# Three norm stages of a one-core transformer block: the norm's products leave GpSimd, and its gain or shift is applied by rows while the transposed tile is split

## The chip, the cores and the metric

The kernel runs on one core of a Trainium2 chip. The metric is the device time of one execution in microseconds (us). Before the change it is 1857.02 us, the median of three runs (1854.01 to 1859.16).

## The reference, cut to what matters

The program computes a two-layer attention block and, on its output, a second block: an even mixer (attention over tokens and a context, and a pooling branch), a mixture of experts (moe 0), an odd mixer (gate and convolution) and a second mixture of experts. x has 512 tokens of 1024 values. The change touches three norms, each of which feeds a matrix product:

```python
def rms_norm(x, g):                      # before layer 2 of the first block
    y = x * lax.rsqrt(jnp.mean(x * x, axis=-1, keepdims=True) + EPS)
    return y * g

def first_block(x, norm_g, w_in, ..., final_g):
    for layer in range(DEPTH):
        h = rms_norm(x, norm_g[layer])
        p = h @ w_in[layer]
        ...
    return rms_norm(x, final_g)          # its output is the x of the second block

def modulate(x, gain, shift, scale):     # before the even and before the odd mixer
    return rms_norm_2(x, gain) * (1 + scale) + shift
```

At the layer boundary the norm has a gain vector and no shift. At the two mixers it has a product vector A = gain * (1 + scale) and a shift vector. The even mixer's norm stands behind the first block's last norm, so there the square sums of x and of x * final_g are both taken.

## The kernel before, in words

The 512 tokens lie in four tiles of 128 tokens by 1024 features, tokens on the partitions. A norm of a tile takes these steps: ScalarE (ACT) squares it and sums the squares; VectorE (DVE) makes the inverse root from the sum by a chain of tiny dependent instructions (`rsqrt_steps`, L376 to L398; DVE executes everything in program order); a product with the vectors follows. The normed tile is then turned: `norm_steps` (L407 to L419) transposes it with TensorE (PE), four 128x128 blocks into one PSUM bank of 128x512, two banks a tile (L414), and `split_to` (L400 to L402) splits each bank in two halves of lower precision: ACT copies the bank into `hT[0]` (hi, L401), and DVE subtracts hi from the bank and writes `hT[1]` (lo, L402). Both are one 128x512 instruction a bank. A product of such operands is three matmuls: hi by hi, hi by lo, lo by hi (L350 to L352).

The three places:

- **Place 1, layer boundary** (`block1_layer`, from L505, 495 to 545 us of the span). `square` (L509) squares on ACT (L512) and has GpSimd (POOL) multiply x with a gain gB that is broadcast to 128 partitions (L513); `turned` (L518) scales that product by the inverse root on ACT (L519). Between them PE finishes layer 1's output product (`w3_`, with DVE's additions at L668), and PE's first products of layer 2 (`latents`, 24 matmuls of 336 columns a tile) follow each tile.
- **Place 2, even mixer** (L1130 to L1245, 985 to 1032 us). `squares(i, engine)` squares x (L1144), multiplies x with final_g in place (L1146; tiles 0 and 1 on DVE, 2 and 3 on POOL), squares again (L1148) and has POOL multiply with A (L1150). `rms` ends with one DVE instruction, product times inverse root plus shift (L1161), where shift is broadcast to 128 partitions. The stage loads ax, gB, pw, ic and psc on SyncE's queue (SP) and scales psc by constants on DVE (L1179, four instructions of 128x1). PE has the last quarter of layer 2's output product (`k.w3`), the context's keys (`project`) and the keys of each tile (`normal`) between the transposes.
- **Place 3, odd mixer** (end of moe 0, L1955 to L2001, 1449 to 1494 us). `added` adds the experts' result (L1968), squares, and multiplies with A1 (tile 0 on DVE, 1 to 3 on POOL); `normed` does product times inverse root plus shift on DVE (L1977).

The order of instructions on all five engines is written by hand in these stages: inside `tc.manual_schedule` the program order is the order of issue, and generators are interleaved by `both` (one step of each in turn), `slow` (one step, then n-1 pauses) and `islice` (the next n steps). Loads go through eight DMA lanes in rotation; an issue on a lane waits for the lane's load before it. `brow` loads a vector of the modulation from DRAM to all 128 partitions.

Of the kernel before, what the change touches and what calls it, by code (L numbers as in the profile page):

```python
# [9 lines left out]
F32 = mybir.dt.float32  # L10
# [222 lines left out]
EARLY = ("e4", "ss2", "rs_y2", "rs_h2", "rs_u2", "T", "V", "ax", "gB", "psc", "pw", "ic", "ss40")  # L233
# [37 lines left out]
class K:  # L271
# [135 lines left out]
    def norm_steps(self, xn, hT, i):  # L407

        nc = self.nc
        for q in range(2):  # L410
# [7 lines left out]
            self.split_to(hT[0][:, ks, c0 : c0 + P], hT[1][:, ks, c0 : c0 + P], src)  # L418
# [32 lines left out]
def block1_layer(k, L, x, hT):  # L451
# [677 lines left out]
def even_mixer(k, x, rows):  # L1129
# [7 lines left out]
    A, sh = brow(k, rows[0], 1), brow(k, rows[0], 0)  # L1137
    us, sss, rss = {}, {}, {}

    def squares(i, engine):  # L1140
# [5 lines left out]
        engine.tensor_tensor(xi, xi, fgB, ALU.mult)  # L1146
        yield
        nc.scalar.activation(u, xi, AF.Square, scale=float(D ** -0.5), accum_out=ss[:, 1:2])  # L1148
        yield
        nc.gpsimd.tensor_tensor(u, xi, A, ALU.mult)  # L1150

    def rms(i):
# [8 lines left out]
        v.scalar_tensor_tensor(us[i], us[i], rss[i][:, 1:2], sh, op0=ALU.mult, op1=ALU.add)  # L1161
# [16 lines left out]
    for b in range(4):  # L1178
        v.tensor_scalar(psc[:, b : b + 1], psc[:, b : b + 1], 0.5 ** (b + 1), None, op0=ALU.mult)  # L1179
# [40 lines left out]
    turned = lambda i: k.norm_steps(us[i], hT, i)  # L1220
    with k.tc.manual_schedule(engines={ENG.PE, ENG.SP, ENG.Pool, ENG.Activation, ENG.DVE}):
        run(project(0))
        k.w3[0]()
        run(squares(0, v))
        k.w3[1]()
        s1, s2, s3 = squares(1, v), squares(2, nc.gpsimd), squares(3, nc.gpsimd)
        both(rms(0), chain(slow(k.w3[2](lambda g: g), 4), islice(s1, 2)))
        run(islice(s2, 2))
        run(s1)
        run(s2)  # L1230
        p1 = project(1)
        both(rms(1), rms(2), chain(slow(k.w3[3](lambda g: g), 2), slow(islice(p1, 1), 2), turned(0)))
        run(islice(s3, 2))
        n0, n1, n2, n3 = (normal(i) for i in range(4))
# [253 lines left out]
def router(k, L):  # L1488
# [7 lines left out]
    for c in range(8):  # L1496
# [6 lines left out]
         "Ab", "pos", "pos16", "most", "over", "oh", "row", "spread", "lgT", "ix", "ws", "vinf", "vpos", "ivx", "ivw",  # L1503
# [13 lines left out]
def moe(k, L, x, tables, out):  # L1517
# [265 lines left out]
    with tc.manual_schedule(engines={ENG.PE, ENG.Pool, ENG.Activation, ENG.DVE}):  # L1783
# [36 lines left out]
        if out is None:  # L1820
            k.next = brow(k, k.rows[1], 1, ("mv", 3)), brow(k, k.rows[1], 0, ("mv", 3))
# [136 lines left out]
    A1, sh1 = k.next  # L1958
# [14 lines left out]
    def normed(i):  # L1973
        v.scalar_tensor_tensor(us[i], us[i], rss[i], sh1, op0=ALU.mult, op1=ALU.add)
# [120 lines left out]
```

## Time and profile before

| | |
|---|---|
| median of three runs | 1857.02 us |
| profiled execution, its own time | 1858.75 us |
| its span | 1857.0 us |
| mean granted TensorE clock | 0.956 |
| busy PE / weight loads / DVE / ACT / POOL | 92 / 72 / 73 / 42 / 15 % |

The profile shows one execution: busy time is the time in which an engine executes, the span is the time from the first instruction to the last. PE can queue matmuls, so two rows of PE that stand one behind the other overlap a little; the distance of their starts is what one costs. A wait on a semaphore is shown as idle time, with the instruction that ended it.

### The profile page before, as it was taken

The numbers are of one execution on the slowest core, as the hardware profiler recorded it, in microseconds if no ns is written. First come the engines' busy times: TensorE is split into PE (matmuls) and PEld (weight loads), VectorE is DVE, ScalarE is ACT, GpSimd is POOL, SyncE is SP. The second block draws the span as 40 slices with busy tenths as digits, with TensorE's granted clock in tenths as the row PEclk, the third lists the DMA queues.
The fourth block names the chain that finished last, engine by engine and source line by source line (L and its number), as shares of the span: only waits on it lengthen the run. The fifth ranks groups of instructions, "written<-read, shape, count | busy, mean of one in ns | idle before, by whom it ended". The sixth has DMA issues, their size and how long they took to land. (4 is left out here: it accounts for less than half of the span.)

```text
span 1857.0 us, 25754 instructions
## 1 busy us (share of the span) xinstructions
PE 1705.9 (92%) x9542; PEld 1334.2 (72%) x9542; DVE 1346.4 (73%) x2532; ACT 770.8 (42%) x1345; POOL 278.2 (15%) x242
## 2 busy tenths in 40 slices
PE   7999999999799999999997889987999799969996
PEld 7877777886697777778866767765666587746663
DVE  4577778876646777576677788879877765589774
ACT  4444333333343443323434445553555322145552
POOL 0000000001200000000003452023221122142221
PEclk9999999999999999999998989997999799979998
DMA  5345565664024445554413213147996463169983
GB/s 176 121 135 149 162 206 162 192 193 135 19 73 125 142 143 151 169 165 148 150 46 110 67 47 126 42 170 265 336 341 194 164 215 95 36 247 304 348 295 75
DMA packets 86948, 298.90 MB, mean 161 GB/s; under 512 B 18854, under 2 KB 20694, under 8 KB 78624
## 3 DMA queue, kind: packets, MB, share of 16 engines
q1 hardware_dynamic: 71584, 271.87, 43.8%
q0 software_dynamic: 10704, 19.79, 4.7%
q10 hardware_dynamic: 4528, 5.51, 1.1%
q8 instruction: 78, 1.28, 0.3%
q14 instruction: 54, 0.44, 0.1%
HBM read 280.23 MB, written 24.96 MB: 164 GB/s over the span
## 5 line engine op out<-in xcount | busy, mean ns | idle before, releaser
L401 ACT ACTIVATE whi<-wraw 128x1024 fp32r<-128x1024 f32 (+2 forms) x166 | 171.7, 1036 | 348.1 <-PE psmm L351 241.6
L350 PE MATMUL psmm<-big,whi 128*128 128x512 f32 x672 | 272.9, 406 | 6.8 <-DVE x L668 5.6
L402 DVE TENSOR_TENSOR wlo<-wraw,whi 128x1024 fp32r<-128x1024 f32 (+3 forms) x165 | 200.9, 1219 | 102.3 <-ACT whi L401 89.6
L352 PE MATMUL psmm<-big,wlo 128*128 128x512 f32 x672 | 266.7, 397 | 0.0
L351 PE MATMUL psmm<-big,whi 128*128 128x512 f32 x672 | 266.6, 397 | 0.0
L980 DVE CUSTOM_DVE_ANT_0 wraw<-wraw,sB 128x1024 f32<-128x1024 f32 x96 | 117.1, 1221 | 83.4 <-DMA wraw<-in_mw_dram 82.9
L350 PE MATMUL psmm<-whi,big 128*128 128x256 f32 (+2 forms) x496 | 165.1, 333 | 1.5 <-ACT big L401 1.0
L351 PE MATMUL psmm<-wlo,big 128*128 128x256 f32 (+2 forms) x496 | 160.7, 324 | 4.9 <-DVE wlo L402 4.9
L352 PE MATMUL psmm<-whi,big 128*128 128x256 f32 (+2 forms) x496 | 159.9, 323 | 2.4 <-DVE big L402 2.3
L350 PEld LDWEIGHTS psmm<-big,whi 128*128 128x128 f32 x672 | 127.3, 189 | 35.8 <-issue 4.7
L352 PEld LDWEIGHTS psmm<-big,wlo 128*128 128x128 f32 x672 | 126.9, 189 | 31.1
L351 PEld LDWEIGHTS psmm<-big,whi 128*128 128x128 f32 x672 | 127.4, 190 | 27.9
L1865 PE MATMUL psmm<-wraw,hs 128*128 128x512 f32 x256 | 122.1, 619 | 5.4 <-ACT hs L1857 3.5
L601 POOL DMA_DIRECT2D qk<-rope x40 | 20.5, 515 | 659.2 <-ACT whi L401 286.9
L351 PEld LDWEIGHTS psmm<-wlo,big 128*128 128x128 f32 x496 | 112.1, 226 | 6.2 <-DVE wlo L402 6.0
L352 PEld LDWEIGHTS psmm<-whi,big 128*128 128x128 f32 x496 | 111.5, 225 | 3.2 <-DVE big L402 3.2
L350 PEld LDWEIGHTS psmm<-whi,big 128*128 128x128 f32 x496 | 111.4, 225 | 2.7 <-ACT big L401 1.7
L350 PE MATMUL pss<-whi,xTh 128*128 128x512 f32 x256 | 104.8, 409 | 2.4 <-ACT xTh L401 2.4
L352 PE MATMUL pss<-whi,xTl 128*128 128x512 f32 x256 | 102.4, 400 | 1.7 <-DVE xTl L402 1.7
L351 PE MATMUL pss<-wlo,xTh 128*128 128x512 f32 x256 | 103.4, 404 | 0.0
L856 PEld LDWEIGHTS pspt<-c_ident,pr 128*128 128x128 f32 x512 | 61.3, 143 | 48.2 <-issue 28.9
L402 DVE TENSOR_TENSOR wlo<-bigm,whi 128x1024 fp32r<-128x1024 f32 x64 | 77.9, 1223 | 17.7 <-ACT whi L401 16.2
(384 smaller groups left out, 3659.7 us busy)
## 6 DMA issues: line engine op xcount, KB each, us to landing
wraw<-in_mw_dram SPq DMA_DIRECT2D x96, 512.0 KB
big<-in_me_dram SPq DMA_DIRECT2D x32, 1024.0 KB
bigm<-in_me_dram SPq DMA_DIRECT2D x32, 1024.0 KB
wraw<-in_me_dram SPq DMA_DIRECT2D x64, 512.0 KB
wraw<-in_wqk_dram SPq DMA_DIRECT2D x48, 512.0 KB
wraw<-in_wv_dram SPq DMA_DIRECT2D x24, 512.0 KB
wraw<-in_ow_dram SPq DMA_DIRECT2D x20, 512.0 KB
wraw<-in_wg_dram SPq DMA_DIRECT2D x16, 512.0 KB
```

What stands on the lines that cost most here:

```text
L350: mm(out, lhs[0], rhs[0], start=first, stop=False)
L351: mm(out, lhs[0], rhs[1], start=False, stop=False)
L352: mm(out, lhs[1], rhs[0], start=False, stop=last)
L401: self.nc.scalar.activation(hi, src, AF.Copy)
L402: (sub or self.nc.vector).tensor_tensor(lo, src, hi.bitcast(F32), ALU.subtract)
L601: nc.gpsimd.dma_start(tiles[b][48:80, :], R[b // 4][32 * (b % 4) : 32 * (b % 4) + 32, :])
L856: nc.tensor.transpose(pt[:, j * P : (j + 1) * P], hd.pr[i][:, j * P : (j + 1) * P], ident)
L980: nc.vector.tensor_tensor_reduce(w, w, sB, 1.0, 0.0, ALU.mult, ALU.add, mf[:, j : j + 1])
L1865: nc.tensor.matmul(acc, hs[:, c * P : (c + 1) * P], w[:, c * 512 : (c + 1) * 512], start=c == 0, stop=c == 1)
```

## The change

At place 1, POOL's product goes. ACT scales x itself by the inverse root (L528 of the changed kernel), and the gain is applied after the transposition, where a feature is a partition: the gain is loaded as `gC`, 128 partitions by 8, and `norm_steps` takes it as `gain`. A bank is then split in four pieces of 128x128, since each of its four blocks has another column of gC: ACT makes hi as piece times gain (L424), DVE makes lo as piece times gain minus hi (L425). At places 2 and 3, POOL's products go as well: x * final_g is DVE's for all four tiles (L1165), product and inverse root are one DVE instruction (L1177, and `normed`), and the shift is applied in the split in the same way, with `shift` (L427, L428) from a 128x8 table `shC`, which takes the place of the broadcast shift. The scalings of psc are written in `pool_mix`. All three stages have a new order of steps.

```diff
-    def norm_steps(self, xn, hT, i):
+    def norm_steps(self, xn, hT, i, gain=None, shift=None):
...
-            self.split_to(hT[0][:, ks, c0 : c0 + P], hT[1][:, ks, c0 : c0 + P], src)
+            if gain is None and shift is None:
+                self.split_to(hT[0][:, ks, c0 : c0 + P], hT[1][:, ks, c0 : c0 + P], src)
+            for j in range(0 if gain is None and shift is None else 4):
+                c = 4 * q + j
+                hi, lo = (h[:, c, c0 : c0 + P] for h in hT)
+                if gain is not None:
+                    nc.scalar.activation(hi, src[:, j, :], AF.Copy, scale=gain[:, c : c + 1])
+                    nc.vector.scalar_tensor_tensor(lo, src[:, j, :], gain[:, c : c + 1], hi.bitcast(F32), op0=ALU.mult, op1=ALU.subtract)
+                else:
+                    nc.scalar.activation(hi, src[:, j, :], AF.Identity, bias=shift[:, c : c + 1])
+                    nc.vector.scalar_tensor_tensor(lo, src[:, j, :], shift[:, c : c + 1], hi.bitcast(F32), op0=ALU.add, op1=ALU.subtract)
...
-        gB = t([P, D], "v4", 10)
-        nc.sync.dma_start(gB, I["norm_g"][L : L + 1, :].to_broadcast([P, D]))
+        gC = t([P, 8], "gC", 1)
+        nc.sync.dma_start(gC, I["norm_g"][L : L + 1, :].rearrange("o (c p) -> p (o c)", p=P))
...
-            nc.gpsimd.tensor_tensor(u, x[:, i, :], gB, ALU.mult)
...
-            nc.scalar.activation(us[i], us[i], AF.Copy, scale=rss[i])
-            return k.norm_steps(us[i], hT, i)
+            nc.scalar.activation(us[i], x[:, i, :], AF.Copy, scale=rss[i])
+            return k.norm_steps(us[i], hT, i, gain=gC)
...
-    A, sh = brow(k, rows[0], 1), brow(k, rows[0], 0)
+    A = brow(k, rows[0], 1)
+    shC = t([P, 8], "shC", 1)
+    nc.sync.dma_start(shC, rows[0][0:1, :].rearrange("o (c p) -> p (o c)", p=P))
...
-        engine.tensor_tensor(xi, xi, fgB, ALU.mult)
-        yield
+        v.tensor_tensor(xi, xi, fgB, ALU.mult)
         nc.scalar.activation(u, xi, AF.Square, scale=float(D ** -0.5), accum_out=ss[:, 1:2])
-        yield
-        nc.gpsimd.tensor_tensor(u, xi, A, ALU.mult)
...
-        v.scalar_tensor_tensor(us[i], us[i], rss[i][:, 1:2], sh, op0=ALU.mult, op1=ALU.add)
+        v.scalar_tensor_tensor(us[i], x[:, i, :], rss[i][:, 1:2], A, op0=ALU.mult, op1=ALU.mult)
...
-    for b in range(4):
-        v.tensor_scalar(psc[:, b : b + 1], psc[:, b : b + 1], 0.5 ** (b + 1), None, op0=ALU.mult)
...
     def pool_mix(b):
+        v.tensor_scalar(psc[:, b : b + 1], psc[:, b : b + 1], 0.5 ** (b + 1), None, op0=ALU.mult)
...
-            k.next = brow(k, k.rows[1], 1, ("mv", 3)), brow(k, k.rows[1], 0, ("mv", 3))
+            shC = small([P, 8], "shC")
+            nc.sync.dma_start(shC, k.rows[1][0:1, :].rearrange("o (c p) -> p (o c)", p=P))
+            k.next = brow(k, k.rows[1], 1, ("mv", 3)), shC
...
-        (nc.gpsimd if i else v).tensor_tensor(us[i], x[:, i, :], A1, ALU.mult)
...
-        v.scalar_tensor_tensor(us[i], us[i], rss[i], sh1, op0=ALU.mult, op1=ALU.add)
+        v.scalar_tensor_tensor(us[i], x[:, i, :], rss[i], A1, op0=ALU.mult, op1=ALU.mult)
```

In the rows below `pspt` is a PSUM bank of transposes, `big` the two halves of hT, `v` and `e` a tile that is being normed, `rs_` and `ss` the inverse root's chain; in brackets stand the semaphores that an instruction waits for (PE_49, DVE_49, Activation_49 and Pool_49 are those of the engines, DMAHWn_49 those of the DMA lanes).

ACT at the layer boundary, before:

```order
L519 ACTIVATE v_947_4428<-v_947_4428,rs_y_950_4433 128x1024 [waits DVE_49,Pool_49]
L512 ACTIVATE v_963_4495,ss_4496<-x 128x1024 [waits DVE_49,Activation_49]
L519 ACTIVATE v_955_4461<-v_955_4461,rs_y_959_4475 128x1024 [waits DVE_49,Pool_49]
L401 ACTIVATE big_77<-pspt_4526 128x4x128 [waits PE_49]
L401 ACTIVATE big_77<-pspt_4534 128x4x128 [waits PE_49]
```

and with the change:

```order
L528 ACTIVATE v_947_4428<-x,rs_y_950_4432 128x1024 [waits DVE_49,Activation_49]
L522 ACTIVATE v_955_4461,ss_4462<-x 128x1024 [waits PE_49]
L424 ACTIVATE big_77<-pspt_4493,gC_4388 128x128 [waits DMAHW3_49,PE_49]
L424 ACTIVATE big_77<-pspt_4493,gC_4388 128x128 [waits DVE_49] x3
L528 ACTIVATE v_955_4461<-x,rs_y_959_4473 128x1024 [waits Activation_49]
L522 ACTIVATE v_964_4507,ss_4508<-x 128x1024
L424 ACTIVATE big_77<-pspt_4518,gC_4388 128x128 [waits PE_49]
L424 ACTIVATE big_77<-pspt_4518,gC_4388 128x128 [waits DVE_49] x3
```

One copy of a bank has become four, of which the second to the fourth wait for DVE, and the wait for POOL has gone.

DVE in the even mixer, tile 0's inverse root, before:

```order
L393 TENSOR_TENSOR rs_u_1897_8868<-rs_y_1895_8866 128x2 [waits DVE_49]
L1146 TENSOR_TENSOR x<-x,e_1870_8755 128x1024 [waits Activation_49]
L1179 TENSOR_SCALAR psc_8770<-psc_8770 128x1 [waits DMAHW5_49]
L1179 TENSOR_SCALAR psc_8770<-psc_8770 128x1 x3
L395 TENSOR_TENSOR rs_u_1897_8868<-rs_u_1897_8868,rs_h_1896_8867 128x2 [waits DVE_49]
L397 SCALAR_TENSOR_TENSOR rs_y_1895_8866<-rs_u_1897_8868,rs_y_1895_8866 128x2 [waits DVE_49]
L1161 SCALAR_TENSOR_TENSOR e_1890_8833<-e_1890_8833,rs_y_1895_8866,e_1872_8759 128x1024 [waits DMAHW7_49,DVE_49,Pool_49]
```

and with the change:

```order
L393 TENSOR_TENSOR rs_u_1899_8910<-rs_y_1897_8908 128x2 [waits DVE_49]
L1313 TENSOR_SCALAR psc_8814<-psc_8814 128x1 [waits DMAHW5_49]
L1313 TENSOR_SCALAR psc_8814<-psc_8814 128x1
L395 TENSOR_TENSOR rs_u_1899_8910<-rs_u_1899_8910,rs_h_1898_8909 128x2 [waits DVE_49]
L1313 TENSOR_SCALAR psc_8814<-psc_8814 128x1 x2
L397 SCALAR_TENSOR_TENSOR rs_y_1897_8908<-rs_u_1899_8910,rs_y_1897_8908 128x2 [waits DVE_49]
L393 TENSOR_TENSOR rs_u_1899_8910<-rs_y_1897_8908 128x2 [waits DVE_49]
L395 TENSOR_TENSOR rs_u_1899_8910<-rs_u_1899_8910,rs_h_1898_8909 128x2 [waits DVE_49]
L397 SCALAR_TENSOR_TENSOR rs_y_1897_8908<-rs_u_1899_8910,rs_y_1897_8908 128x2 [waits DVE_49]
L1177 SCALAR_TENSOR_TENSOR e_1890_8873<-x,rs_y_1897_8908,e_1871_8801 128x1024 [waits DMAHW6_49,DVE_49]
L1165 TENSOR_TENSOR x<-x,e_1870_8799 128x1024 [waits Activation_49]
L428 SCALAR_TENSOR_TENSOR big_8798<-pspt_8936,shC_8803,big_8797 128x128 [waits DMAHW7_49,Activation_49]
```

The scalings of psc still stand in tile 0's chain, one round earlier in it, and their first still waits for a DMA lane; tile 1's product with final_g now stands behind tile 0's product, ahead of its split.

DVE in the even mixer, between tile 1's and tile 2's transposes, before:

```order
L397 SCALAR_TENSOR_TENSOR rs_y_1904_8915<-rs_u_1906_8917,rs_y_1904_8915 128x2 [waits DVE_49]
L1161 SCALAR_TENSOR_TENSOR e_1899_8885<-e_1899_8885,rs_y_1904_8915,e_1872_8759 128x1024 [waits DVE_49,Pool_49]
L397 SCALAR_TENSOR_TENSOR rs_y_1907_8920<-rs_u_1909_8922,rs_y_1907_8920 128x2
L1161 SCALAR_TENSOR_TENSOR e_1901_8893<-e_1901_8893,rs_y_1907_8920,e_1872_8759 128x1024 [waits DVE_49,Pool_49]
L402 TENSOR_TENSOR big_8754<-pspt_9013,big_8753 128x4x128 [waits Activation_49]
L402 TENSOR_TENSOR big_8754<-pspt_9020,big_8753 128x4x128 [waits Activation_49]
```

and with the change:

```order
L428 SCALAR_TENSOR_TENSOR big_8798<-pspt_9052,shC_8803,big_8797 128x128 [waits Activation_49] x4
L397 SCALAR_TENSOR_TENSOR rs_y_1915_9045<-rs_u_1917_9047,rs_y_1915_9045 128x2 [waits DVE_49]
L428 SCALAR_TENSOR_TENSOR big_8798<-pspt_9066,shC_8803,big_8797 128x128 [waits Activation_49] x4
L393 TENSOR_TENSOR rs_u_1917_9047<-rs_y_1915_9045 128x2 [waits DVE_49]
L395 TENSOR_TENSOR rs_u_1917_9047<-rs_u_1917_9047,rs_h_1916_9046 128x2 [waits DVE_49]
L397 SCALAR_TENSOR_TENSOR rs_y_1915_9045<-rs_u_1917_9047,rs_y_1915_9045 128x2 [waits DVE_49]
L1177 SCALAR_TENSOR_TENSOR e_1901_8933<-x,rs_y_1915_9045,e_1871_8801 128x1024 [waits DVE_49]
```

Tile 2's product (L1161, L1177 now) stood ahead of tile 1's split and now stands behind all eight pieces of it.

## Rows read from the trace of the kernel before

**Rows 1.** The page: busy time of each engine over the span, its share, instructions.

```profile
PE 1705.9 (92%) x9542; PEld 1334.2 (72%) x9542; DVE 1346.4 (73%) x2532; ACT 770.8 (42%) x1345; POOL 278.2 (15%) x242
```

**Rows 2.** Windows, place 2: length, busy us by engine (instructions), granted clock, DMA.

```profile
core 0: us, PE busy (x) PEld busy (x) DVE busy (x) ACT busy (x) POOL busy (x), PEclk, DMA share, GB/s
1000.00:1032.00 32.00, 20.92 (x137) 19.61 (x136) 23.73 (x79) 12.58 (x29) 11.74 (x8) 0.73 0.28 95
```

**Rows 3.** Waits of PE, places 1, 2, 3: us in total, times, longest.

```profile
PE pspt L414 <- DVE big L402: 5.6, 1, 5.6
...
PE pspt L414 <- DVE ss L1155: 7.3, 1, 7.3
...
PE pspt L414 <- DVE rs_v L384: 4.8, 1, 4.8
```

**Rows 4.** Groups by line and form: count, busy us, mean ns of one, idle before.

```profile
L401 ACT ACTIVATE big<-pspt 128x512 fp32r<-128x512 f32 x32 | 17.9, 593 | 27.2 <-PE pspt L414 27.1
L731 ACT ACTIVATE v<-pspt,gs 128x512 fp32r<-128x512 f32 x10 | 6.4, 686 | 8.8 <-PE pspt L729 8.8
L1216 ACT ACTIVATE T<-psmm 128x128 f32<-128x128 f32 x4 | 1.1, 278 | 5.3 <-PE psmm L352 5.3
...
L402 DVE TENSOR_TENSOR big<-pspt,big 128x512 fp32r<-128x512 f32 x32 | 21.1, 685 | 11.6 <-ACT big L401 11.3
L1764 DVE TENSOR_TENSOR pr<-pss,pr 128x256 f32<-128x256 f32 x32 | 13.5, 423 | 0.8
L732 DVE SCALAR_TENSOR_TENSOR v<-pspt,gs,v 128x512 fp32r<-128x512 f32 x10 | 7.1, 746 | 2.1 <-ACT v L731 2.1
```

**Rows 5.** Timeline, place 2, DVE then ACT: start, us, instruction, idle before.

```profile
991.11 1.23 DVE L1146 TENSOR_TENSOR x<-x,e 128x1024 f32<-128x1024 f32 x1 [1.22 <-ACT e L1144]
...
992.37 1.07 ACT L1148 ACTIVATE e<-x 128x1024 f32<-128x1024 f32 x1 [1.29 <-DVE x L1146]
```

**Rows 6.** Timeline, place 1, POOL and DVE.

```profile
496.29 2.40 POOL L513 TENSOR_TENSOR v<-x,v 128x1024 f32<-128x1024 f32 x1 [8.55 <-ACT v L512]
...
497.16 1.56 DVE L391 SCALAR_TENSOR_TENSOR rs_u<-rs_y,rs_h 128x1 f32<-128x1 f32 x1
```

**Rows 7.** Timeline, place 2, DMA issues of ACT and SP, then DVE.

```profile
986.84 0.35 ACTq L1097 DMA_DIRECT2D ctx_kv<-v  x1
...
1002.61 0.33 SPq L1177 DMA_DIRECT2D psc<-in_psc_dram  x1
...
1005.05 0.34 DVE L1179 TENSOR_SCALAR psc<-psc 128x1 f32<-128x1 f32 x4 [6.04 <-DMA psc<-in_psc_dram]
...
1006.16 1.28 DVE L1161 SCALAR_TENSOR_TENSOR e<-e,rs_y,e 128x1024 f32<-128x1024 f32 x1
```

**Rows 8.** DMA packets in 989 to 1003, 990 to 991 and 993 to 1000 us.

```profile
DMA packets 1881, 0.88 MB, mean 63 GB/s; under 512 B 1481, under 2 KB 1737, under 8 KB 1881
...
DMA packets 269, 0.07 MB, mean 67 GB/s; under 512 B 268, under 2 KB 269, under 8 KB 269
...
DMA packets 538, 0.17 MB, mean 24 GB/s; under 512 B 494, under 2 KB 522, under 8 KB 538
```

**Rows 9.** Timeline, the ends of the three places: DVE's last splits, PE's marks.

```profile
522.21 1.29 DVE L402 TENSOR_TENSOR big<-pspt,big 128x512 fp32r<-128x512 f32 x2 [3.29 <-ACT big L401]
...
529.06 0.31 PE L352 MATMUL psmm<-whi,big 128*128 128x336 f32 x1
...
1020.09 1.18 PE L414 MATMUL pspt<-c_ident,e 128*128 128x128 f32 x8
...
1026.16 1.06 PE L414 MATMUL pspt<-c_ident,e 128*128 128x128 f32 x8 [0.66 <-DVE e L1161]
...
1031.19 0.28 PE L352 MATMUL psmm<-whi,big 128*128 128x256 f32 x1
...
1479.30 1.28 DVE L402 TENSOR_TENSOR big<-pspt,big 128x512 fp32r<-128x512 f32 x2
...
1493.55 0.28 PE L352 MATMUL psmm<-whi,big 128*128 128x256 f32 x1
1493.66 0.39 PE L350 MATMUL psmm<-big,whi 128*128 128x512 f32 x1
```

More of the change, by code (lines that the diff above doesn't have):

```diff
@@ L232 @@
 LATE = ("v4", "sB", "gk", "ss8", "ss", *(f"rs_{c}{n}" for c in "vyhu" for n in "1n"))
-EARLY = ("e4", "ss2", "rs_y2", "rs_h2", "rs_u2", "T", "V", "ax", "gB", "psc", "pw", "ic", "ss40")
+EARLY = ("e4", "shC", "ss2", "rs_y2", "rs_h2", "rs_u2", "T", "V", "ax", "gB", "psc", "pw", "ic", "ss40")
 QK_ORDER = ((0, 0), (0, 1), (0, 2), (1, 1), (1, 2), (1, 0))
@@ L1219, in even_mixer, with turned @@
     project, scale, keys = k.ctx
-    turned = lambda i: k.norm_steps(us[i], hT, i)
+    def turned(i):
+        yield from k.norm_steps(us[i], hT, i, shift=shC)
     with k.tc.manual_schedule(engines={ENG.PE, ENG.SP, ENG.Pool, ENG.Activation, ENG.DVE}):
@@ L1223, in even_mixer @@
         k.w3[0]()
-        run(squares(0, v))
+        s0, s1, s2, s3 = (squares(i) for i in range(4))
+        run(s0)
         k.w3[1]()
-        s1, s2, s3 = squares(1, v), squares(2, nc.gpsimd), squares(3, nc.gpsimd)
-        both(rms(0), chain(slow(k.w3[2](lambda g: g), 4), islice(s1, 2)))
-        run(islice(s2, 2))
+        run(islice(s1, 1))
+        both(rms(0), slow(k.w3[2](lambda g: g), 5))
         run(s1)
+        run(islice(s2, 1))
+        t0, t1, t2, t3 = (turned(i) for i in range(4))
+        p1 = project(1)
+        n0, n1, n2, n3 = (normal(i) for i in range(4))
+        run(islice(t0, 1))
+        both(rms(1), slow(k.w3[3](lambda g: g), 5))
+        run(t0)
         run(s2)
[L1231 to L1234, printed above, removed]
+        run(islice(p1, 1))
         run(islice(n0, 1))
         run(islice(s3, 1))
-        run(turned(1))
+        both(rms(2), chain(repeat(None, 4), t1))
+        run(s3)
         run(n0)
-        run(s3)
         run(p1)
-        both(rms(3), scale(), chain(repeat(None, 6), turned(2)))
+        both(rms(3), scale(), chain(repeat(None, 6), t2))
         run(n1)
         run(islice(n2, 1))
-        run(turned(3))
+        run(t3)
         run(n2)
@@ L1502 @@
 SMALL = ("lg", "sm", "cmp", "rank", "G", "lgr", "gm", "ge", "gsum", "e2", "w1", "w2", "sec", "We", "Ws",
-         "Ab", "pos", "pos16", "most", "over", "oh", "row", "spread", "lgT", "ix", "ws", "vinf", "vpos", "ivx", "ivw",
+         "Ab", "pos", "pos16", "most", "over", "oh", "row", "spread", "lgT", "ix", "ws", "vinf", "vpos", "ivx", "ivw", "shC",
          "rs_v2", "rs_y2", "rs_h2", "rs_u2")
@@ L1957, in moe @@
     k.hT = hT = [t([P, 8, 512], "big", 2, F32R) for _ in range(2)]
-    A1, sh1 = k.next
+    A1, shC = k.next
     rss.clear()
@@ L1984, in moe @@
             k.split_to(yh[:, ns], yl[:, ns], y[:, ns])
+        turn_ = lambda i: k.norm_steps(us[i], hT, i, shift=shC)
         run(added(0))
-        run(added(1))
-        both(rms(0, 1), added(2))
+        both(rms(0, 1), slow(added(1), 3))
         normed(0)
-        both(rms(1, 1), added(3))
-        k.transpose_norm(us[0], hT, 0)
+        both(rms(1, 1), slow(added(2), 3))
+        t0, t1 = turn_(0), turn_(1)
+        run(islice(t0, 1))
         normed(1)
-        both(rms(2, 1), rms(3, 1))
-        k.transpose_norm(us[1], hT, 1)
+        run(t0)
+        both(rms(2, 1), slow(added(3), 3))
+        run(islice(t1, 1))
         normed(2)
-        k.transpose_norm(us[2], hT, 2)
+        run(t1)
+        t2, t3 = turn_(2), turn_(3)
+        both(rms(3, 1), slow(t2, 3))
         normed(3)
         k.ahead.append(k.weights(I["ow"], 2048, 1024))
-        k.transpose_norm(us[3], hT, 3)
+        run(t3)
 def body(tc, I, out, stop=None):
```

32 lines of the change are left out of this document (20 added, 12 removed).

## The prediction

> **What bounds the kernel now.** First the page: PE is busy for 92% of the span, no other engine for more than 73% [rows 1]. So an engine that is not PE costs time only where PE waits for it, and the next view is the list of PE's waits at the three places. There the reader sees one long wait at each: 5.6 us at place 1, 7.3 at place 2, 4.8 at place 3, each at the transposes L414, each for DVE [rows 3]. DVE is the bound of all three stages; POOL counts only as far as it holds up DVE or ACT. In the window of place 2 PE is busy for 20.92 of 32 us and its granted clock is 0.73, between 1.2 and 2.4 GHz, so there PE both waits and works slowly [rows 2]. Third, the timeline of DVE tells what it does while PE waits. At place 1 a tiny instruction of the inverse root takes 1.56 us while POOL's product of 2.40 us runs [rows 6]. At place 2 DVE itself stands idle for 6.04 us for psc, whose load SP issues only at 1002.61 although it stands in a list that began over ten microseconds before; a store of the context, ctx_kv, was issued at 986.84 and holds the lane [rows 7].
>
> **The price of a bank.** The change does the split in four pieces of 128x128 on each of ACT and DVE, 96 pieces in all (3 places, 4 tiles, 2 banks, 4 pieces). I first took ACT to run ahead and DVE to follow. The order rows say otherwise: ACT's second, third and fourth piece of a bank each wait for DVE, and each of DVE's pieces waits for ACT. So hi, lo, hi, lo alternate, and a bank costs four round trips between the engines. The trace of before has no such alternation within a bank; its price is built from rows. ACT's 128x128 from PSUM takes 0.278 us, and an operand per partition adds up to 0.09 (686 against 593 ns for 128x512). DVE's 128x128 is an estimate: 685 ns at 512 columns and 423 at 256 make 1.02 ns a column, so some 0.29 at 128, and with the operand per partition (746 against 685) up to 0.35 [rows 4]. A hop from DVE to ACT is 992.37 - (991.11 + 1.23) = 0.03 [rows 5]. A round trip is then 0.28 + 0.03 + 0.29 + 0.03 = 0.63 at least and 0.37 + 0.03 + 0.35 + 0.03 = 0.78 at most; I take 0.72, since both operands are there and only their full price is doubtful. From a bank's first lo to its last, DVE is tied for three trips and one piece, 2.5 us (2.2 to 2.7); before, it was one instruction of 0.69. Nothing else of DVE gets in between, as it works in order. Eight banks a place: 8 x (2.5 - 0.69) = +14.5 us of DVE at each place. This is the change's main cost.
>
> The Trainium skill explains the waits: its page "PSUM — Partial Sum Buffer", section "PSUM bank collisions raise a hardware error", says that two engines may not touch one bank at once, reads included, so that the compiler puts a dependency between them even for different columns. It speaks against this change. Without it, ACT would run ahead and a bank would tie DVE for four pieces only, 4 x 0.33 = 1.3 us, +5 a place instead of +14.5; the semaphores of the changed program agree with the page, so I go by them.
>
> **Place 1.** Removed: four POOL products and with them the slow instructions of DVE's chain and PE's 5.6 us [rows 3, 6]. Added: +14.5 of DVE. The last lo stood at 522.21 + 1.29 = 523.5 [rows 9]; it comes at 523.5 - 5.6 + 14.5 = 532.4. Before, PE had 5.7 us of latents left behind it, to 529.2 (the row at 529.06 is the last one of tile 3; such matmuls start 0.155 apart); now PE keeps up with DVE's pieces, so latents end 0.3 behind the last lo, at 532.7: +3.5. The next weights' lo (L402) queue behind DVE's last piece: +1.3. **+4.8** (1 to 7 with trips of 0.63 to 0.78). gC's load is issued in layer 1, some 70 us ahead: nothing.
>
> **Place 2.** The wait for psc stays: the second order fence shows psc's scalings in the same chain, an iteration earlier, behind the same lane. From psc's landing at 1005.05 [rows 7] DVE then has in its queue: the rest of the chain 1.3 (1.1 by rows, and a step more), the product of tile 0 1.2, x*final_g of tile 1 1.2, a wait for ACT's square of tile 1, and first hi 2.5 (1.07, its sum's read, transposes, a hi), bank 0 2.4, the chain of tile 1 and two additions of w3 3.8 (PE's w3[3] now stands between bank 0 and bank 1), the product 1.2, bank 1 2.4, x*final_g of tile 2 1.2 (POOL's before), its square on ACT 1.2, the start of tile 2's chain 1.8, both banks of tile 1 5.1, the end of the chain 1.3, the product 1.2. Sum 27.8: tile 2 can be transposed at 1032.8, before at 1020.09 [rows 9], +12.7. The third order fence is the decisive piece: tile 2's product used to stand ahead of tile 1's split. From there to tile 3's transposes it was 6.1 us (1026.16 - 1020.09); now two banks with first hi and transposes 6.9, the chain's rest 3.4 and the product 1.2, 11.5: a further +5.4. From there to the last matmul of the keys at 1031.19 it was 5.1; with 5.4 for two banks instead of 1.3, partly beside matmuls, it is 7.7: +2.6. **+20.7** (14 to 26). The removed POOL products release some of DVE's stalls, which I have counted as gone: all prices above are undisturbed ones.
>
> **The load of shC.** It reads 1024 single floats, feature by feature, into 128x8, and it is issued ahead of the loads up to psc. If it goes in as many packets as it has elements, psc's lane comes free later by 1024 divided by the queues' rate. In 989 to 1003 us 1481 packets under 512 B moved in 14 us, 106 a us: 9.7 us. The fastest of those microseconds has 268: 3.8 us; the stretch from 993 to 1000 has 494 in 7 us, 71 a us: 14.5 us [rows 8]. The broadcast of shift that goes had 128 packets, about 1 us. So **+8.5** by the mean of the very stretch in which it runs, between +2.5 and +13.5, and 0 if it moves in few packets. No row of before shows such a load by itself. The Trainium skill, "DMA: Bandwidth & Descriptors", section "Rules for kernel authors", says that a strided last dimension becomes one descriptor per element; by that the term is 2.5 to 13.5 and without it 0. The second shC, in moe 0, is issued on SP ahead of weights that have some 19 us of slack: nothing, at most +5 if SP's queue waits for it.
>
> **Place 3.** The wait of 4.8 goes with its cause, POOL's products beside the chain [rows 3], and about 1.5 of slow tiny instructions. Added: +14.5 of DVE. The last split ends at 1479.30 + 1.28 = 1480.6 [rows 9], now 8.2 later, at 1488.8. Before, 13.1 us of matmuls followed to the first 128x512 at 1493.66; they start 0.11 apart (1493.55, 1493.66) [rows 9]. About 120 such matmuls of 256 columns still lie behind the last split, 14 us at the fast level: 1502.8, up to 1506 if they start at the slow one. **+11** (9 to 15).
>
> **Sum.** 4.8 + 20.7 + 8.5 + 11 = +45. On the profiled execution's 1858.75 that is 1903.8; it stands 1.7 above the median of the runs shown, so the prediction is **1902 us**. About 0.3% of the time, 5.6 us, is what can be told from no change. A tenth of a microsecond in the round trip is 8 to 10 us in the sum, the largest single doubt.
>
> **Rivals.**
> 1. *The alternation is cheap, and the removed waits count* (faster). The place: the four pieces of a bank. If a round trip cost no more than 0.3 us, DVE would be tied for 1.2 us a bank, less than now with POOL's disturbance, and PE's waits of 5.6 and 4.8 would go without anything in their place, place 2 staying as it is for psc: 1858.75 - 10.4 - 1.7 = 1846.6. For it: the rows on POOL's disturbance are real [rows 6]. Against it: ACT's piece alone is 0.278 in the trace [rows 4]. It decides at a trip of about 0.3. Chance 0.06.
> 2. *Short trips and a quick shC* (slower by less). Trips of 0.63 make the places 2.6, 15 and 9.4, and shC lands in the shadow of other loads, +1: +28, 1885. For it: the 128x128 row on ACT and the slope on DVE are the plain readings. Against: both pieces carry a pointer operand. Chance 0.22.
> 3. *Long trips and a slow shC*: 7 + 24 + 15 + 13.5 = +59.5, 1916.5; with a late load in moe 0 up to 1921. For it: 993 to 1000 is just the stretch in which the element loads would run. Chance 0.17.
> 4. *No change that can be told*: the delays at each place are covered by a lateness that is there anyway (psc at place 2, the weights' splits behind places 1 and 3), and the removed waits pay for the rest: 1857, within 5.6 either way. Against: behind all three places PE's matmuls need hT first. Chance 0.05.
>
> **Numbers.** My forecast, with trips near 0.72 and shC near the mean rate, is 1893 to 1911, chance 0.50; with rivals 2 and 3 the range 1876 to 1920 leaves out rivals 1 and 4 and the outer ends. Faster 0.06, same 0.05, slower 0.89 (forecast, 2, 3).
>
> **What would show it.** Right: groups L424, L425, L427, L428 with 96 pieces each over two lines, ACT's and DVE's idle time before them ended by one another, starts of DVE's pieces in one bank 0.6 to 0.8 apart; the last lo of place 1 at about 532, PE's transposes of tile 2 at place 2 some 20 us later than before (12.7 and 8.5), psc landing at about 1013; the first 128x512 matmul of place 3 later by some 45. Wrong: pieces of ACT that overlap DVE's in one bank, trips under 0.5, psc landing at or before 1005 plus what place 1 shifts, or PE busy through these stretches, so that another engine's lateness costs nothing.

## The result, and the profile after

The changed kernel takes 1898.62 us (median of four runs, 1895.72 to 1901.6) against 1855.97 us for the kernel before in the same runs: a ratio of 1.0228, 95% interval [1.0201, 1.0255], slower by 42.7 us. The forecast was 1902 us. The sum came out within 4 us, yet two of its terms were off by 10 and by 5 us in opposite directions, so the closeness of the total is partly luck.

The page's first lines after the change, beside [rows 1]:

```profile
span 1899.8 us, 25878 instructions
...
PE 1717.2 (90%) x9542; PEld 1339.0 (70%) x9542; DVE 1349.5 (71%) x2605; ACT 789.2 (42%) x1417; POOL 248.1 (13%) x229
```

PE does the same 9542 instructions. Of the 43 us by which the span grows, 11 are a longer busy time of PE for them (1717.2 against 1705.9, at a mean granted clock of 0.950 against 0.956), and the other 32 are idle time of PE. DVE is busy for only 3 us more than before, although DVE was the bound at all three places: what DVE spends in addition is idle time, and a view of busy shares would not have shown it.

The waits of PE at places 1, 2 and 3 (495 to 540, 1000 to 1060 and 1470 to 1545 us; in total, times, longest), which answer to [rows 3]:

```profile
PE pspt L414 <- ACT v L528: 7.8, 3, 4.7
...
PE pspt L414 <- DVE e L1177: 25.6, 4, 11.8
PE pspt L414 <- DVE big L428: 2.0, 1, 2.0
...
PE psmm L350 <- ACT PT L366: 5.4, 1, 5.4
```

At place 2, where the longest wait was 7.3 us, the tiles now wait for DVE for 25.6 us in four waits; the one at place 1 has changed its owner (ACT's scaling, which stands behind ACT's pieces). The pieces themselves, grouped by line (count, busy us, mean ns, idle before):

```profile
L427 ACT ACTIVATE big<-pspt,shC 128x128 fp32r<-128x128 f32 x64 | 22.5, 366 | 35.2 <-DVE big L428 29.0 <-PE pspt L414 6.1
L428 DVE SCALAR_TENSOR_TENSOR big<-pspt,shC,big 128x128 fp32r<-128x128 f32 x64 | 22.2, 350 | 27.4 <-ACT big L427 27.4
L424 ACT ACTIVATE big<-pspt,gC 128x128 fp32r<-128x128 f32 x32 | 11.6, 366 | 13.4 <-DVE big L425 13.4
L425 DVE SCALAR_TENSOR_TENSOR big<-pspt,gC,big 128x128 fp32r<-128x128 f32 x32 | 11.1, 350 | 15.2 <-ACT big L424 15.2
```

Each engine's idle time before its pieces is ended by the other engine: 29.0 + 13.4 us on ACT, 27.4 + 15.2 on DVE. One bank at place 2 on DVE's and on ACT's timeline (start, us, instruction, idle before):

```profile
1014.79 0.35 DVE L428 SCALAR_TENSOR_TENSOR big<-pspt,shC,big 128x128 fp32r<-128x128 f32 x1 [2.51 <-ACT big L427]
1015.58 0.35 DVE L428 SCALAR_TENSOR_TENSOR big<-pspt,shC,big 128x128 fp32r<-128x128 f32 x1 [0.44 <-ACT big L427]
1016.36 0.35 DVE L428 SCALAR_TENSOR_TENSOR big<-pspt,shC,big 128x128 fp32r<-128x128 f32 x1 [0.44 <-ACT big L427]
1017.15 0.35 DVE L428 SCALAR_TENSOR_TENSOR big<-pspt,shC,big 128x128 fp32r<-128x128 f32 x1 [0.44 <-ACT big L427]
```

```profile
1014.40 0.35 ACT L427 ACTIVATE big<-pspt,shC 128x128 fp32r<-128x128 f32 x1
1015.17 0.37 ACT L427 ACTIVATE big<-pspt,shC 128x128 fp32r<-128x128 f32 x1 [0.42 <-DVE big L428]
1015.96 0.37 ACT L427 ACTIVATE big<-pspt,shC 128x128 fp32r<-128x128 f32 x1 [0.42 <-DVE big L428]
```

DVE's starts are 0.79 apart: 0.37 for ACT, 0.35 for DVE, two hops of some 0.035. That is one round trip, and a bank ties DVE for 3 x 0.785 + 0.35 = 2.7 us.

psc at place 2, which answers to [rows 7]: the store's issue on ACT, the list's last issue on SP, DVE.

```profile
991.66 0.35 ACTq L1114 DMA_DIRECT2D ctx_kv<-v  x1
...
1007.01 0.33 SPq L1193 DMA_DIRECT2D psc<-in_psc_dram  x1
...
1008.76 0.22 DVE L1313 TENSOR_SCALAR psc<-psc 128x1 f32<-128x1 f32 x2 [7.92 <-DMA psc<-in_psc_dram]
```

and the loads of that list, 985 to 1010 us (KB each, us from issue to landing):

```profile
gB<-in_qkg_dram SPq DMA_DIRECT2D x1, 256.0 KB, 16.0
pw<-in_pw_dram SPq DMA_DIRECT2D x1, 256.0 KB, 16.2
...
ctx_kv<-v ACTq DMA_DIRECT2D x1, 64.0 KB, 15.3
...
shC<-mrow SPq DMA_DIRECT2D x1, 4.0 KB, 5.0
psc<-in_psc_dram SPq DMA_DIRECT2D x1, 2.0 KB, 1.7
```

The wait for psc is there as forecast, but DVE has psc 17.1 us behind the issue of ctx_kv, before 18.2: shC's elements landed in 5.0 us beside the others, and no delay of psc by them shows. Slow are gB's larger load and those issued behind it; the runs with another load of gB below tell which of them is the cause.

Where the 43 us come from is best read from three lengths in each trace. Place 1 is from ACT's first square to the first 512-column product of layer 2; place 2 from ctx_kv's issue to the transposes behind the last key product; place 3 from the first product with spread to the first 128x512 product behind it. They are differences of starts on the timelines, in us; the runs below stand in the same table.

| kernel | place 1 | place 2 | place 3 | ratio to before [95%] |
|---|---|---|---|---|
| before | 49.0 | 44.5 | 48.3 | 1 |
| changed | 55.4 | 64.1 | 63.8 | 1.0228 [1.0201, 1.0255] |
| hi_first | 46.9 | 53.7 | 51.7 | 1.0078 [1.0049, 1.0106] |
| wide | 46.0 | 50.0 | (not comparable) | (not comparable) |
| no_shc2 | 55.2 | 63.7 | (not comparable) | (not comparable) |
| psc_first | 55.4 | 56.6 | 61.7 | 1.0217 [1.0193, 1.0242] |
| dve_wide | 44.2 | 56.0 | 49.2 | 1.0056 [1.0036, 1.0076] |
| dve_wide_gb | 44.2 | 49.5 | 48.6 | 0.9998 [0.9984, 1.0011] |
| hi_first_gb | 47.0 | 46.1 | 54.0 | 1.0023 [1.0006, 1.0040] |
| gb_before | 48.1 | 44.5 | 47.6 | 0.9984 [0.9968, 1.0000] |
| mixed | 44.2 | 42.4 | 48.0 | 0.9960 [0.9944, 0.9975] |
| mixed_slow_gb | 44.2 | 49.5 | 47.5 | 1.0002 [0.9992, 1.0012] |
| mixed_p3 | 45.8 | 42.5 | 46.1 | 0.9952 [0.9935, 0.9969] |

The change costs 6.4 + 19.6 + 15.5 = 41.5 us at its three places, of the 42.9 by which the two profiled executions differ (1901.6 and 1858.75). Each length comes from one execution. Where two kernels have the same code at a place, their lengths differ by up to 1.6 us at place 1 (mixed and mixed_p3), 0.1 at place 2 (mixed and mixed_p3) and 2.3 at place 3 (hi_first and hi_first_gb), so smaller differences than these decide nothing.

### The profile page after: what moved, and what is told of

The parts are those of the page before. It is cut to its first block, busy times and chain, and to the rows that moved or that the text cites. A ratio compares the mean times of both kernels' runs of the same rounds, so it can differ in the third digit from the quotient of the medians.

```text
span 1899.8 us, 25878 instructions
## 1 busy us (share of the span) xinstructions
PE 1717.2 (90%) x9542; PEld 1339.0 (70%) x9542; DVE 1349.5 (71%) x2605; ACT 789.2 (42%) x1417; POOL 248.1 (13%) x229
## 2 busy tenths in 40 slices
DMA packets 89637, 297.34 MB, mean 157 GB/s; under 512 B 21926, under 2 KB 23766, under 8 KB 81312
## 3 DMA queue, kind: packets, MB, share of 16 engines
q8 instruction: 78, 1.28, 0.3%
## 5 line engine op out<-in xcount | busy, mean ns | idle before, releaser
L350 PE MATMUL psmm<-whi,big 128*128 128x256 f32 (+2 forms) x496 | 170.3, 343 | 9.3 <-ACT PT L366 5.4
L352 PE MATMUL psmm<-whi,big 128*128 128x256 f32 (+2 forms) x496 | 164.0, 331 | 0.2 <-DVE big L428 0.2
L350 PEld LDWEIGHTS psmm<-whi,big 128*128 128x128 f32 x496 | 115.1, 232 | 13.4 <-ACT PT L366 5.8
L352 PEld LDWEIGHTS psmm<-whi,big 128*128 128x128 f32 x496 | 114.8, 232 | 1.3 <-DVE big L428 0.4
L873 PEld LDWEIGHTS pspt<-c_ident,pr 128*128 128x128 f32 x512 | 61.0, 142 | 48.0 <-issue 28.2
```

What stands on the lines that cost most here:

```text
L350: mm(out, lhs[0], rhs[0], start=first, stop=False)
L352: mm(out, lhs[1], rhs[0], start=False, stop=last)
L873: nc.tensor.transpose(pt[:, j * P : (j + 1) * P], hd.pr[i][:, j * P : (j + 1) * P], ident)
```

## The experiments

**hi_first** takes the alternation away and nothing else: the four hi of a bank stand ahead of its four lo.

```diff
-            for j in range(0 if gain is None and shift is None else 4):
+            for half, j in ((h, j) for h in range(0 if gain is None and shift is None else 2) for j in range(4)):
...
-                if gain is not None:
+                if gain is not None and half == 0:
                     nc.scalar.activation(hi, src[:, j, :], AF.Copy, scale=gain[:, c : c + 1])
+                elif gain is not None:
                     nc.vector.scalar_tensor_tensor(lo, src[:, j, :], gain[:, c : c + 1], hi.bitcast(F32), op0=ALU.mult, op1=ALU.subtract)
...
```

> The changed kernel, with the four hi pieces of a bank ahead of its four lo pieces; the same 768 instructions, loads and order of steps. Theory A (the cost of the change is the alternation of ACT and DVE within a PSUM bank, 0.785 us a round trip in its trace): a bank ties DVE for four pieces one behind the other, some 1.1 us, in place of 2.7, while its first lo comes about 0.8 later; of the 43 us that the change costs, 20 to 30 go: 1869 to 1879 us. Rival B (the new order of steps, with the products of POOL on DVE, is the cost): within 6 us of the changed kernel's 1898.6. Rival C (the loads of single elements, gC and shC, are the cost): also within 6 us of it.

It takes 1871.36 us, 27 us less than the changed kernel. A bank in its trace, ACT's and DVE's row:

```profile
1011.61 1.12 ACT L428 ACTIVATE big<-pspt,shC 128x128 fp32r<-128x128 f32 x4
```

```profile
1012.76 1.13 DVE L430 SCALAR_TENSOR_TENSOR big<-pspt,shC,big 128x128 fp32r<-128x128 f32 x4 [3.28 <-ACT big L428]
```

Four pieces in a row cost 1.13 us on DVE (one adds 0.26) in place of 2.7. With the same instructions, loads and order of steps, 27 of 43 us are gone: theory A holds for that part, and B and C, which allowed 6, do not explain it. Places 1 and 3 are at 46.9 and 51.7; place 2 keeps 9 us.

**wide** goes back to one 128x512 instruction an engine and bank.

```diff
-            if gain is None and shift is None:
+            if True:
...
-            for j in range(0 if gain is None and shift is None else 4):
+            for j in range(0):
```

> The changed kernel with the old split, one 128x512 instruction on ACT and one on DVE a bank; it leaves out the gain at the layer boundary and the shift at the two mixers, but keeps their loads, the products on DVE and the new order of steps. Theory A: all of the pieces' cost goes, and with POOL's products out of the way places 1 and 3 are even shorter than before the change: 1846 to 1858 us. Rival B: the order alone keeps it above 1880. Rival C: above 1880 too, as the loads are still there.

Without gain and shift the later stages work on other numbers: the program runs 40134 instructions in place of 25878 and takes 4314.85 us, so nothing behind place 2 can be read. Ahead of that, place 1 takes 46.0 us, 3 less than before, and place 2 takes 50.0. So at place 1 the pieces took 9.5 us, and the rest of the change (the new order and POOL's product gone) gains; at place 2 the pieces cost 14.1, and the new order together with POOL's products on DVE costs 5.5. Theory A is right for the larger part there; how much of the rest is the order, as B has it, this run does not tell (mixed_slow_gb does).

**dve_wide** asks the same question with the whole computation kept: the changed order, wide split, vectors on DVE ahead of the transposes.

```diff
-            nc.scalar.activation(us[i], x[:, i, :], AF.Copy, scale=rss[i])
-            return k.norm_steps(us[i], hT, i, gain=gC)
+            nc.vector.scalar_tensor_tensor(us[i], x[:, i, :], rss[i], gB, op0=ALU.mult, op1=ALU.mult)
+            return k.norm_steps(us[i], hT, i)
...
         v.scalar_tensor_tensor(us[i], x[:, i, :], rss[i][:, 1:2], A, op0=ALU.mult, op1=ALU.mult)
+        v.tensor_tensor(us[i], us[i], sh, ALU.add)
...
         v.scalar_tensor_tensor(us[i], x[:, i, :], rss[i], A1, op0=ALU.mult, op1=ALU.mult)
+        v.tensor_tensor(us[i], us[i], sh1, ALU.add)
```

> The changed order of steps with the split as it was before the change, one 128x512 instruction on each engine a bank. Gain and shift are applied ahead of the transposition on DVE: the layer boundary's product is one instruction x times root times broadcast gain, the two mixers have one addition of the broadcast shift more a tile (8 of 1.2 us); no POOL products, no loads of single elements. Theory A (the pieces in the bank are the cost): place 1 in 46 to 48 us from the first square to the first 512-column product (before 49.0, changed 55.4), place 2 in 51 to 55 (44.5, 64.1), place 3 in 48 to 52 (48.3, 63.8), in all 1855 to 1866 us. Rival B (the order of steps is the cost): places 2 and 3 stay within 4 us of the changed kernel's, in all over 1880.

It takes 1868.81 us, 9.5 more than before in the same runs (1859.34): 1865.5 on the base of the other runs, the upper end of theory A's range and far from B's. Place 1 is even below its range (44.2), place 3 in it (49.2), place 2 one above it (56.0). At place 3 the changed kernel takes 14.7 us more than this one: that is what the pieces cost there beyond the additions that replace them. Without them the place is back within 0.9 us of before.

**no_shc2** replaces the load of single elements at the same place in the queue.

```diff
-    nc.sync.dma_start(shC, rows[0][0:1, :].rearrange("o (c p) -> p (o c)", p=P))
+    nc.sync.dma_start(shC[:, 0:4], I["psc"])
+    v.memset(shC[:, 4:8], 0.0)
```

> The changed kernel without the even mixer's load of single elements: shC is loaded from psc's rows (128 packets) on the same lane and at the same place in SP's queue, so this kernel leaves out the even mixer's true shift. The prediction's term: psc lands 2.5 to 13.5 us earlier against the issue of ctx_kv, 8.5 by its choice, and the time falls by as much, to about 1890. Rival (the load of 1024 elements runs beside the others, and the lane comes free when a slow load that was there before lets ctx_kv through): psc lands within 2 us of where it did, 17.1 us behind the issue of ctx_kv, and the time stays within 4 us of 1898.6.

Again only the stretch up to place 2 can be read: without the true shift the whole takes 3135.83 us. psc reaches DVE 17.0 us behind ctx_kv's issue (1007.68 and 990.67), with the load of elements 17.1; place 2 lasts 63.7 us, with it 64.1. The rival is right: the prediction's term of 8.5 is nothing here, where gB's load is on its way beside shC's.

**psc_first** issues psc ahead of the list.

```diff
+    psc = t([P, 4], "psc", 1)
+    nc.sync.dma_start(psc, I["psc"])
     A = brow(k, rows[0], 1)
...
-    psc = t([P, 4], "psc", 1)
-    nc.sync.dma_start(psc, I["psc"])
```

> The changed kernel with psc's load issued first of the even mixer's list, so that DVE's 7.92 us of idle time for it go. Theory (place 2 is a queue of DVE's work that begins when psc lands): all that is behind it comes earlier by 5 to 8 us, so 1891 to 1894 us. Rival (another wait stands ready, ACT's squares or PE's products): less than 3 us of gain, and the wait that took its place stands in DVE's list.

The 7.92 us of idle time are gone from DVE's list of waits, and no other wait has taken their place there: place 2 lasts 56.6 us in place of 64.1, 7.5 less, as the theory has it. The time is 1895.43, only 3.2 less than the changed kernel's; the interval of its ratio overlaps that of the changed kernel, so the gain in time is not settled. In the two traces the transposes behind the last key product come 4.5 us earlier, counted from place 1's end (501.0 and 505.4 us behind it), because the stretch between places 1 and 2 is 3.0 us longer in this execution. That is not the edit's doing: the list's first load, final_g's, which SP issues ahead of psc's, already comes 3.0 us later (441.0 and 437.9 us behind place 1's end). Why that stretch took longer was not found.

**gb_before** and **hi_first_gb** load gB as two rows and spread it on POOL.

```diff
-        nc.sync.dma_start(gB[:, h0 : h0 + nh, :], I["qkg"][r : r + 1, :].unsqueeze(1).to_broadcast([P, nh, 64]))
+        nc.sync.dma_start(gB[:, h0, :], I["qkg"][r : r + 1, :].to_broadcast([P, 64]))
...
+    for h0, nh in ((0, 2), (2, 8)):
+        nc.gpsimd.tensor_copy(gB[:, h0 + 1 : h0 + nh, :], gB[:, h0 : h0 + 1, :].to_broadcast([P, nh - 1, 64]))
     finish(0, 6)
```

> The kernel before the change, with one edit: gB is loaded as its two rows of 64 (256 packets) and spread to ten on POOL just ahead of its use, in place of 1280 packets. Theory (the slow packets that keep ctx_kv's store, and so psc's lane, waiting 15 us are gB's): psc is issued within 4 us of ctx_kv, DVE's 6.04 us of idle time for it go, and 3 to 6 us of the time: 1850 to 1853 us. Rival (ctx_kv's own packets are the slow ones): psc is issued some 15 us behind ctx_kv as before, the time is within 1.5 us of before. Second rival (psc comes early, but POOL's products hold the stage just as long): psc early, less than 2 us gained.

> The changed kernel with the four hi pieces of a bank first (1871.4 us) and the same edit of gB. Theory: as DVE's queue at place 2 begins when psc lands, 5 to 7 us of the stage's 53.7 go, 1864 to 1867 us. Rival (another wait stands ready behind psc's): less than 3 us.

In both, ctx_kv lands in 5.0 and 4.1 us in place of 15.3, and DVE does not wait for psc. Two of gb_before's loads:

```profile
pw<-in_pw_dram SPq DMA_DIRECT2D x1, 256.0 KB, 5.0
...
ctx_kv<-v ACTq DMA_DIRECT2D x1, 64.0 KB, 5.0
```

So gB's load was the cause. The edit takes away packets and bytes together: 1280 packets become 256 (the page of gb_before counts 17831 packets under 512 B, that of before 18854), and 320 KB become 64. The times differ. hi_first_gb takes place 2 from 53.7 to 46.1 us, a little more than the 5 to 7 expected (ratio from 1.0078 to 1.0023). gb_before leaves place 2 at 44.5, as the second rival has it; its ratio of 0.9984 has an interval from 0.9968 to 1, so a gain of up to 6 us in time is not excluded. DVE and POOL of gb_before, in the stretch that was the wait for psc:

```profile
994.98 2.33 DVE L395 TENSOR_TENSOR rs_u<-rs_u,rs_h 128x2 f32<-128x2 f32 x1
997.34 2.27 DVE L397 SCALAR_TENSOR_TENSOR rs_y<-rs_u,rs_y 128x2 f32<-128x2 f32 x1
999.71 3.26 DVE L1161 SCALAR_TENSOR_TENSOR e<-e,rs_y,e 128x1024 f32<-128x1024 f32 x1
```

```profile
994.10 3.19 POOL L1146 TENSOR_TENSOR x<-x,e 128x1024 f32<-128x1024 f32 x1 [2.07 <-ACT e L1144]
997.25 4.64 POOL L1150 TENSOR_TENSOR e<-x,e 128x1024 f32<-128x1024 f32 x2
```

Instructions that take 0.15 us elsewhere take 2.3 beside POOL's products, and 1.28 becomes 3.26. DVE used to idle for psc in just that time; now it is held, and tile 0 is ready at the same point: L1161 ends 20.6 us behind ctx_kv's issue in both kernels.

**dve_wide_gb** joins that edit with dve_wide.

> The changed order with the wide split and the vectors on DVE (ratio 1.0056), and gB in 256 packets. With no POOL product at place 2 nothing fills the time in which psc was waited for, so the gain is as large as in the changed order with the hi pieces first (7.5 us there): place 2 from 56.0 to 48 or 49 us, in all 5 to 8 us less, ratio 1.001 to 1.003. Rival (the additions on DVE have become the bound of place 2): 2 us or less.

Place 2 goes from 56.0 to 49.5 us, the ratio from 1.0056 to 0.9998: without POOL's products the wait for psc is worth 6.5 us. PE still waits there for DVE (985 to 1040 us):

```profile
PE pspt L414 <- DVE e L1176: 15.9, 4, 7.5
```

**mixed** puts together the best of each place, and **mixed_slow_gb** undoes its edit of gB. Of mixed's edits, those of place 2 (that of gB is gb_before's, that of place 1 as in dve_wide):

```diff
-        engine.tensor_tensor(xi, xi, fgB, ALU.mult)
+        v.tensor_tensor(xi, xi, fgB, ALU.mult)
...
-        nc.gpsimd.tensor_tensor(u, xi, A, ALU.mult)
...
-        v.scalar_tensor_tensor(us[i], us[i], rss[i][:, 1:2], sh, op0=ALU.mult, op1=ALU.add)
+        v.scalar_tensor_tensor(us[i], x[:, i, :], rss[i][:, 1:2], A, op0=ALU.mult, op1=ALU.mult)
+        v.tensor_tensor(us[i], us[i], sh, ALU.add)
```

> The kernel before the change with three edits: place 1 in the changed order with the wide split and x times root times broadcast gain on DVE; place 2 in the order of before with gB in 256 packets and no POOL product (final_g for all tiles, and an addition of the broadcast shift a tile, on DVE); place 3 as before. Theory (psc's wait and POOL's hold on DVE's tiny instructions lie side by side at place 2, so only both together gain): place 1 at 44 us (before 49.0), place 2 at 38 to 42 (44.5 before, and with the one edit of gB), place 3 at 48; in all 7 to 11 us less than before, ratio 0.994 to 0.996. Rival (DVE's own work is what place 2 lasts): place 2 at 44 or more, ratio 0.997.

> The kernel named mixed with gB loaded as before, in 1280 packets: the fourth corner beside before (POOL's products, slow gB: place 2 lasts 44.5 us), gb_before (POOL's products, quick gB: 44.5) and mixed (no POOL products, quick gB: 42.4). Theory (the wait for psc and POOL's hold on DVE lie side by side, so taking away one of the two gains nothing, and DVE's additions then cost): place 2 at 45 to 50 us with DVE idle for psc for 6 us or more, ratio 0.997 to 1.000. Rival (gB never mattered in this order; the 2 us came from POOL's products alone): 42 to 43 us.

mixed is faster than both kernels, by 0.4% against before, 0.9960 [0.9944, 0.9975], at the end of the expected ratios; place 2 takes 42.4 us, just outside 38 to 42. mixed_slow_gb is at 1.0002, its place 2 at 49.5, and DVE idles for psc again:

```profile
1007.73 0.34 DVE L1186 TENSOR_SCALAR psc<-psc 128x1 f32<-128x1 f32 x4 [7.12 <-DMA psc<-in_psc_dram]
```

The four corners of place 2, in the order of before: POOL's products with slow gB 44.5, POOL's products with quick gB 44.5, no POOL products with slow gB 49.5, neither 42.4. At place 2 each edit alone gains nothing or loses; only both gain. These runs also price the new order of steps: at place 2, dve_wide and mixed_slow_gb have the same instructions in the two orders, and so have dve_wide_gb and mixed. The new order takes 56.0 against 49.5 and 49.5 against 42.4 us, so it costs 6.5 to 7.1 us there, beside the pieces.

**mixed_p3** takes POOL's products out of place 3 as well.

```diff
-        (nc.gpsimd if i else v).tensor_tensor(us[i], x[:, i, :], A1, ALU.mult)
...
-        v.scalar_tensor_tensor(us[i], us[i], rss[i], sh1, op0=ALU.mult, op1=ALU.add)
+        v.scalar_tensor_tensor(us[i], x[:, i, :], rss[i], A1, op0=ALU.mult, op1=ALU.mult)
+        v.tensor_tensor(us[i], us[i], sh1, ALU.add)
```

> The kernel named mixed, with place 3 in the order of before but without POOL's products: x times root times A1, and an addition of the broadcast shift, on DVE for all tiles. Removed: POOL's hold on DVE's chain, part of PE's wait of 4.8 us; added: three products' worth, 3.7 us, of DVE. Theory (DVE is place 3's bound, so the two nearly cancel): place 3 at 46 to 50 us, ratio within 0.0015 of mixed. Rival (POOL's hold is the larger by far): place 3 under 45.

Place 3 goes from 48.0 to 46.1, less than the 2.3 us by which equal code differs there; the ratio is 0.9952 [0.9935, 0.9969]. That is as the theory had it, and with mixed the fastest here, though the two can't be told apart.

## Why the prediction was right, and where it was not

- **The price of a bank.** Right in its mechanism, and the largest term: the alternation was read from the semaphores of the changed program and priced from [rows 4, 5] at 0.63 to 0.78 us a trip. 0.72 was taken, 0.785 measured; the upper end was the true one, as both pieces took what the estimate with the operand's full price gives (366 and 350 ns). hi_first shows that the alternation is the cause of 27 us. The Trainium skill, "PSUM — Partial Sum Buffer", section "PSUM bank collisions raise a hardware error", says that a dependency is put between two engines' accesses to one bank, reads included; the traces agree as far as the waits go, which end one another in every bank. What two reads at once would do was not tried.
- **Place 1.** Forecast +4.8, measured +6.4, within the range of 1 to 7 that longer trips gave. The last lo starts at 533.29, forecast to end at 532.4.
- **Place 2 from psc's landing.** Forecast +20.7. Measured from psc on DVE to the transposes behind the keys: 1055.72 - 1008.76 = 46.96 us, before 1031.31 - 1005.05 = 26.26, so +20.7. The steps on the way were forecast at 27.8, 11.5 and 7.7 us and came at 28.2 (tile 2's transposes at 1036.91), 11.8 (tile 3's at 1048.72) and 7.0. A bank cost 2.7 us there where 2.5 was taken, so the sum is equal only because other steps were priced too high; which ones was not worked out.
- **The load of shC.** The step that failed. It was sized by the mean rate of packets in [rows 8], +8.5, and it is -1.1 in the trace (17.1 against 18.2) and nothing in no_shc2. It did move one packet an element: the page counts 21926 packets under 512 B, before 18854, and 3 x 1024 is the difference. The Trainium skill, "DMA: Bandwidth & Descriptors", section "Rules for kernel authors", says that a strided last dimension becomes one descriptor per element; the count agrees. The error was to take a rate for a capacity: those 106 packets a microsecond were what went by while gB's slow load was on its way, with room beside it. After the change, while shC's load was on its way, 935 packets moved in 2 us (991 to 993):

```profile
DMA packets 935, 0.62 MB, mean 311 GB/s; under 512 B 766, under 2 KB 790, under 8 KB 935
```

  One of the prediction's own signs of being wrong thus came: psc was in use at 1008.76, where 1005.05 and the 4.8 us by which ctx_kv's issue was later make 1009.9; the forecast had it landing at about 1013.
- **Place 3.** Forecast +11 (9 to 15), measured +15.5, just outside. The last split ends 46.9 us behind the place's first product, before 35.3: +11.6 where 8.2 was taken. Of the 3.4 missing, 1.4 is DVE's longer wait for x from DRAM at the start (its first addition stands 5.7 us behind the first product, before 4.3), and 1.6 is the longer bank, 8 x 0.2; 0.4 was not found. The rest lies behind the last split:

```profile
1481.00:1494.00 13.00, 13.00 (x114) 12.93 (x113) 5.69 (x8) 5.88 (x9) 0.00 (x0) 1.00 0.74 235
```

```profile
1518.00:1523.00 5.00, 4.60 (x21) 4.61 (x22) 1.27 (x3) 1.40 (x2) 0.00 (x0) 0.50 0.77 239
1518.00:1535.00 17.00, 16.60 (x121) 16.61 (x122) 6.32 (x10) 6.08 (x9) 0.00 (x0) 0.84 0.46 137
```

  The first is the window from the last split to the place's end before, the third that of the changed kernel, and the second its first 5 us (PE, PEld, DVE, ACT, POOL busy, granted clock, DMA share, GB/s). Before, PE came to it busy and ran at 2.4 GHz throughout. Now it comes from a wait of 5.4 us; the granted clock is 0.50, so 1.2 GHz, in the first 5 us, and 0.84 in the mean. "1506 if they start at the slow one" was the right case.
- **The sum.** 45 forecast, 42.9 measured between the profiled executions: 9.6 too much at shC, 1.6 + 4.5 too little at places 1 and 3, and 1.4 outside the places. That the errors nearly cancel is luck.
- **The rivals.** The first (pieces that cost no more than 0.3 us a trip) is out, as trips cost 0.785; but its gain was real: with the alternation gone, place 1 is 2 to 5 us below before. The forecast's own pair, trips of 0.72 and a slow shC, did not come: the long trips are those of rival 3, the quick shC that of rival 2, and together they give nearly the same sum.

## What to carry to other kernels

When two engines read one PSUM bank, write all of one engine's pieces ahead of the other's: the same work cost 27 us less here than in pieces that take turns. Where a stage has two causes of delay side by side, each must be tried with the other taken away; here neither psc's wait nor POOL's products showed alone. And the rate at which packets go by is no capacity: before an added load is priced by it, look for the transfer that makes the stretch slow.

## What was not expected of the hardware

The slow load at place 2 was 256 KB of gB, one row of 64 floats repeated 8 times for each of 128 partitions in 1024 packets: 16.0 us from issue to landing, while pw with the same 256 KB issued behind it took 16.2, ctx_kv 15.3 and ic 14.2. With gB's two loads in 128 packets each, pw landed in 5.0, ctx_kv in 5.0 and ic in 4.7. With gB's load as it was, the others of its list thus took three times as long, but not shC's 1024 elements, which were issued ahead of it and landed in 5.0. The bytes alone do not explain it, as pw's 256 KB landed in 5.0. Whether it is the number of small packets, the repeated address or the way that the packets are spread over the DMA engines was not tried.
